# Narrow dilated attention: the values product as high and low parts at full width, with one raw buffer

## The chip, the cores and the metric

The kernel runs on one core of a Trainium2 chip. The metric is the device time of one execution in microseconds; three runs of the kernel before took 2870.96, 2873.74 and 2878.09 us, median 2873.74 us.

## The reference, cut to what matters

The program is two transformer blocks over 1024 tokens of width 1024, in float32. The second block has two attentions: a latent attention (8 heads) and a mixture of three dilated window attentions. The change touches two of the three dilated groups. Group g has 8 heads of 64 dimensions and dilation r = 1, 4 or 16; a query sees keys at offsets m*r with |m| <= 64:

```python
for g, (window, dilation) in enumerate(((128, 1), (512, 4), (2048, 16))):
    o, lse = dilated_group(q[:, :, sl], k[:, :, sl], v[:, :, sl], dilation, window // (2 * dilation))
# in dilated_group, per block of queries and its neighbourhood of keys:
s = where(valid, q @ k.T * D ** -0.5, NEG_INF)
m = max(s); p = exp(s - m); den = sum(p)
o = (p @ v) / den;  lse = m + log(den)
```

The groups' outputs are then mixed with a softmax over their lse.

## The kernel before, in words

Most of the kernel's work is projections. To keep float32 accuracy with float32r matmuls, both operands are split into a high part (a copy rounded to float32r, on ScalarE, L153) and a low part (the difference, on VectorE, L154), and three matmuls high x high, high x low, low x high are summed (L187 to L189). `kk.split` does the splitting.

The projections also serve as fill: `kk.fill` queues generators of projection matmuls, and `kk.pump(amount)` issues from them until the amount is used up (one step of three 512-column matmuls counts 3.0). The attention stages are traced in program order with a pump between their steps. The order of instructions on each engine is fixed before the run by a planner, which goes by priority (program order, with some blocks raised or lowered) and by when it expects an instruction's inputs and buffers to be ready; at run time each engine then works its queue strictly in that order and waits on semaphores.

The narrow dilated groups are computed by `dil_attention` (L1253), first for g = 1 (dilation 4, per = 12), then for g = 0 (dilation 1, per = 11). The widest group has a function of its own and isn't touched. Heads are taken in pairs, m = 0 to 3; the two heads of a pair lie on partitions 0 to 63 and 64 to 127. A unit (m, u) is two blocks of 128 queries of one pair; there are 16 units per group. For one unit:

- `scores` (L1314): 12 matmuls (64 rows each, the two heads side by side in the array) give for each of 4 (block, head) cells 256 key columns in PSUM; VectorE adds the mask and takes the maximum (L1334), ScalarE the exponential with its sum (L1336), into `d_p`.
- `turn` (L1340), once per head: four 128x128 transposes by TensorE (L146) into the one PSUM bank `pT`, then one copy into `d_pT`: on ScalarE for the first head (L1348), on VectorE for the second (L1346).
- `values` (L1353): 8 float32 matmuls into the bank `pO` (L1360), 128 keys by 64 value dimensions by 128 queries. Head 0 writes partitions 0 to 63, head 1 partitions 64 to 127. In the profile each stands as two records. In group 0 two neighbouring query blocks share the middle one of three key blocks; in group 1 both use the same two key blocks. ScalarE copies the result out (L1365, or L1370 with a stride for g = 1), and it is stored.

The loop (L1382) issues for each unit: transposes of head 0, a piece of preparation (queries at u = 0 and 2, keys of the next pair at u = 1, the load of the pair after next at u = 3), the next unit's scores, a pump, transposes of head 1, the values product of the unit before, and a pump. `load(m)` (L1269) loads keys, queries and values of a pair into double buffers (`dk_raw`, `dq_raw`, `dv`); two pairs are loaded before the loop. In group 0 GpSimd writes zeros into the two half blocks of values at the ends. `prep_k` (L1290) and `prep_q` (L1303) split keys and queries.

The forgetting attention of the first block and the latent attention of the second already compute their values product on split operands, with the value's high and low parts side by side in 128 weight columns (L550 to L552, L568) and the two halves of the result added on the way out (`pv_evac`, L521).

Of the kernel before, what the change touches and what calls it, by code (L numbers as in the profile page):

```python
# [1252 lines left out]
def dil_attention(kk, pool, C, g, qT, kT, v_d, od, nm_d, l_d, per):  # L1253
# [15 lines left out]
    def load(m):  # L1269
        rows = slice(m * P, m * P + P)  # L1270
        out = []
        for nm, src in (("dk_raw", kT), ("dq_raw", qT)):
            t = kk.t(pool, [P, S], F32, nm, 2)
            nc.sync.dma_start(t, src[rows, :])
            out.append(t)
        raws[m] = out
        v = kk.t(pool, [P, 9 - g, P], F32, "dv", 2)
        if g == 0:
            nc.gpsimd.memset(v[0:64, 0, :], 0.0)
            nc.gpsimd.memset(v[64:128, 8, :], 0.0)  # L1280
            nc.sync.dma_start(v[64:128, 0, :], v_d[0:64, rows])
            nc.sync.dma_start(v[:, 1:8, :], v_d[64 : 64 + 7 * P, rows].rearrange("(s p) c -> p s c", p=P))
            nc.sync.dma_start(v[0:64, 8, :], v_d[960:1024, rows])
        else:
            src = v_d[:, rows].rearrange("(h p r) c -> r p h c", r=4, p=P)
            for j in range(4):
                nc.sync.dma_start(v[:, 2 * j : 2 * j + 2, :], src[j])
        vals[m] = v

    def prep_k(m):  # L1290
        kh = kk.t(pool, [P, S + 2 * pad], F32R, "dKH", 2)
# [48 lines left out]
    def turn(pr, hh):  # L1340
        pt = kk.pT()
        for j in range(4):
            kk.transpose(pt[:, j * P : j * P + P], pr[:, hh * 512 + j * P : hh * 512 + j * P + P])
        pT = kk.t(pool, [P, 512], F32, "d_pT", 4 - g)
        if hh:
            nc.vector.tensor_copy(pT, pt)  # L1346
        else:
            nc.scalar.copy(pT, pt)  # L1348
        return pT

    outs = {}

    def values(m, u, pTs):  # L1353
        v = vals[m]
        po = kk.pO()
        for j in range(2):
            for w in range(2):
                blk = 2 * u + j + w if g == 0 else 2 * u + w
                for hh in range(2):
                    nc.tensor.matmul(po[half[hh], j * P : j * P + P], v[:, blk, half[hh]],  # L1360
                                     pTs[hh][:, (2 * j + w) * P : (2 * j + w + 1) * P], start=w == 0, stop=w == 1)
        rows = od[m * P : m * P + P, :]
        if g == 0:
            on = kk.t(pool, [P, 256], F32, "d_on", 2)
            nc.scalar.copy(on, po[:, :256])  # L1365
            nc.sync.dma_start(rows[:, u * 256 : u * 256 + 256], on)
            return
        if u == 0:
            outs[m] = kk.t(pool, [P, S], F32, "d_on", 1)
        nc.scalar.copy(perm(outs[m])[:, u, :], po[:, :256])  # L1370
        if u == 3:
            nc.sync.dma_start(rows, outs.pop(m))

    units = [(m, u) for m in range(4) for u in range(4)]
    load(0)
    prep_k(0)
    prep_q(0, 0)
    pr = scores(0, 0)
    load(1)
    kk.pump(40)  # L1380
    held = deque()
    for n, (m, u) in enumerate(units):  # L1382
        cur = pr
        nxt = units[n + 1] if n + 1 < len(units) else None
        pTs = []
        for hh in range(2):
            pTs.append(turn(cur, hh))
            if hh == 0:
                if u == 0:
                    prep_q(m, 1)  # L1390
                elif u == 1 and m < 3:
                    prep_k(m + 1)
                elif u == 2 and m < 3:
                    prep_q(m + 1, 0)
                elif u == 3 and m < 2:
                    load(m + 2)
                if nxt is not None:
                    pr = scores(*nxt)
            elif held:
                values(*held.popleft())  # L1400
            kk.pump(per)
        held.append((m, u, pTs))
    while held:
        values(*held.popleft())
# [380 lines left out]
```

## Time and profile before

| | |
|---|---|
| median of three runs | 2873.74 us |
| the profiled execution | 2867.28 us, span 2865.5 us |
| mean granted clock of TensorE | 0.996 of full |
| TensorE busy | 98% of the span, 14595 matmuls |
| VectorE, ScalarE, GpSimd busy | 44%, 37%, 8% |
| group 1 (g = 1) | about 1941 to 2092 us |
| group 0 (g = 0) | about 2126 to 2270 us |
| float32 values product L1360 | 512 records, 35.0 us busy, 279 ns mean |

How to read it: a record's duration holds the matmul's way through the pipeline, and records overlap; what a matmul costs is the distance from its start to the next one's start. Busy time of an engine is the union of its records. `pO<-d_pT,dv` is out<-in by the program's tile names. Weight loads (PEld) run beside the matmuls.

### The profile page before, as it was taken

Reading aid. Unit: us, or ns where it says so; the run is one execution under the profiler, and the core shown is the slowest. Engines: PE = TensorE matmul, PEld = TensorE weight load, DVE = VectorE, ACT = ScalarE, POOL = GpSimd, SP = SyncE. Lnnn points to the kernel's source line nnn. Section 1 sums busy time; section 2 is a strip of 40 time slices with the busy share of each in tenths; the row PEclk is TensorE's granted clock in tenths of the full one; section 3 lists DMA queues with packets and bytes.
Section 4 is the critical chain, followed back from the end, with each engine's and each line's share of the span. In section 5 each row is a group of like instructions: output and inputs, shape, how many; then the busy total and the mean of one; then the engine's idle time right before and its main releaser. Section 6 shows DMA issues by size and latency. Waiting matters only on the chain.

```text
span 2865.5 us, 37017 instructions
## 1 busy us (share of the span) xinstructions
PE 2814.2 (98%) x14595; PEld 2290.2 (80%) x14595; DVE 1253.8 (44%) x2072; ACT 1069.3 (37%) x1876; POOL 239.7 (8%) x321
## 2 busy tenths in 40 slices
PE   8999999999999999999999899999999999999998
PEld 6887788888888888888888778877777777888787
DVE  7144455545343222222315443535523366555553
ACT  4133555544131111111113331315547655555522
POOL 0012200000000000000000000000000165401100
PEclk9999999999999999999999999999999999999999
DMA  5112643255311111111113264543353355422641
GB/s 169 54 61 75 172 114 110 78 172 195 112 37 45 59 48 55 45 44 45 52 37 108 76 198 121 164 125 112 88 163 98 119 163 157 140 80 76 194 150 59
DMA packets 216327, 298.65 MB, mean 104 GB/s; under 512 B 34180, under 2 KB 137284, under 8 KB 216152
## 3 DMA queue, kind: packets, MB, share of 16 engines
q1 hardware_dynamic: 206104, 267.15, 30.2%
q0 software_dynamic: 10048, 29.13, 3.4%
q8 instruction: 114, 1.87, 0.3%
q14 instruction: 61, 0.50, 0.1%
HBM read 212.73 MB, written 81.36 MB: 103 GB/s over the span
## 4 chain that ended last, share of the span: by engine, by line
PE 93%; DMA 2%; DVE 2%; issue 1%; ACT 1%; POOL 0%; SPq 0%; POOLq 0%; ACTq 0%; DVEq 0%
PE pA L187 10%; PE pA L189 10%; PE pA L188 9%; PE pS L187 9%; PE pS L189 9%; PE pS L188 9%; PE pX L187 8%; PE pX L189 8%; PE pX L188 8%; PE pT L146 4%; PE pO L568 3%; PE pO L1360 1%; PE pS L1325 1%; PE pS L709 1%; PE pS L710 1%
## 5 line engine op out<-in xcount | busy, mean ns | idle before, releaser
L154 DVE TENSOR_TENSOR wl<-wraw,wh 128x1024 fp32r<-128x1024 f32 (+3 forms) x208 | 250.6, 1207 | 282.2 <-ACT wh L153 281.3
L153 ACT CAST wh<-wraw 128x1024 fp32r<-128x1024 f32 (+3 forms) x208 | 213.6, 1031 | 399.5 <-PE pA L189 238.3
L187 PE MATMUL pS<-big,wh 128*128 128x512 f32 x704 | 277.8, 395 | 0.0
L189 PE MATMUL pS<-big,wl 128*128 128x512 f32 x704 | 277.0, 393 | 0.0
L188 PE MATMUL pS<-big,wh 128*128 128x512 f32 x704 | 275.9, 392 | 0.0
L187 PE MATMUL pA<-big,wh 128*128 128x512 f32 x656 | 266.0, 405 | 0.2 <-ACT fm_out L733 0.2
L189 PE MATMUL pA<-big,wl 128*128 128x512 f32 x656 | 259.2, 395 | 0.0
L188 PE MATMUL pA<-big,wh 128*128 128x512 f32 x656 | 258.2, 394 | 0.0
L267 POOL TENSOR_TENSOR rs_r<-rs_v,mhalf 128x1 f32<-128x1 f32 (+3 forms) x64 | 61.3, 959 | 1523.8 <-DVE rs_v L266 1125.6
L154 DVE TENSOR_TENSOR ptl<-pT,pth 128x512 fp32r<-128x512 f32 (+2 forms) x184 | 116.1, 631 | 162.5 <-ACT pth L153 162.1
L187 PE MATMUL pX<-big,wh 128*128 128x512 f32 x432 | 175.0, 405 | 4.7 <-DVE dp L1012 3.5
L187 PE MATMUL pX<-wh,big 128*128 128x512 f32 (+2 forms) x448 | 171.5, 383 | 1.4 <-ACT l_x L1050 1.4
L187 PE MATMUL pA<-wh,big 128*128 128x512 f32 (+2 forms) x448 | 170.6, 381 | 0.0
L189 PE MATMUL pX<-big,wl 128*128 128x512 f32 x432 | 170.2, 394 | 0.0
L189 PE MATMUL pX<-wh,big 128*128 128x512 f32 (+2 forms) x448 | 169.3, 378 | 0.6 <-DVE big L154 0.6
L188 PE MATMUL pX<-big,wh 128*128 128x512 f32 x432 | 169.7, 393 | 0.0
L189 PE MATMUL pA<-wh,big 128*128 128x512 f32 (+2 forms) x448 | 169.3, 378 | 0.0
L188 PE MATMUL pX<-wl,big 128*128 128x512 f32 (+2 forms) x448 | 169.0, 377 | 0.1
L188 PE MATMUL pA<-wl,big 128*128 128x512 f32 (+2 forms) x448 | 168.3, 376 | 0.0
L189 PEld LDWEIGHTS pS<-big,wl 128*128 128x128 f32 x704 | 132.2, 188 | 31.3
L188 PEld LDWEIGHTS pS<-big,wh 128*128 128x128 f32 x704 | 132.5, 188 | 30.4
L187 PEld LDWEIGHTS pS<-big,wh 128*128 128x128 f32 x704 | 132.2, 188 | 29.4 <-ACT big L153 0.2
(426 smaller groups left out, 5736.4 us busy)
## 6 DMA issues: line engine op xcount, KB each, us to landing
wraw<-in_w_in_dram SPq DMA_DIRECT2D x96, 512.0 KB
wraw<-in_w_gate_dram SPq DMA_DIRECT2D x22, 512.0 KB
wraw<-in_w_up_dram SPq DMA_DIRECT2D x22, 512.0 KB
wraw<-in_w_down_dram SPq DMA_DIRECT2D x22, 512.0 KB
wraw<-in_w_out_dram SPq DMA_DIRECT2D x16, 512.0 KB
gT<-fm_out SPq DMA_DIRECT2D x32, 256.0 KB
ld<-gT SPq DMA_DIRECT2D x32, 256.0 KB
dq<-dp SPq DMA_DIRECT2D x96, 64.0 KB
```

What stands on the lines that cost most here:

```text
L146: self.nc.tensor.transpose(out, src, self.ident)
L153: self.nc.scalar.copy(h, src)
L154: self.nc.vector.tensor_tensor(l, src, h.bitcast(F32), op=ALU.subtract)
L187: mm(out, lhs[0], rhs[0], start=start, stop=False)
L188: mm(out, lhs[0], rhs[1], start=False, stop=False)
L189: mm(out, lhs[1], rhs[0], start=False, stop=stop)
L267: nc.gpsimd.tensor_tensor(r[:, :n], v[:, :n], self.mhalf[:, :n], op=ALU.pow)
L568: nc.tensor.matmul(po[:, c0:256], v2[:, kb + j, :], pr[m][:, j, c0:], start=kb == 0 and j == 0 and m == 0, stop=last and j == 1 and m == 1)
L709: nc.tensor.matmul(ps[:, c0:c1], q2[:, qs], k2[:, c0:c1], start=True, stop=False)
L710: nc.tensor.matmul(ps[:, c0:c1], qb[:, qs], kb_[:, c0:c1], start=False, stop=not last)
L1325: nc.tensor.matmul(ps[:, o : o + 256], q[half[hh], q0 : q0 + P], k[half[hh], k0 : k0 + 256], start=i == 0, stop=i == 2)
L1360: nc.tensor.matmul(po[half[hh], j * P : j * P + P], v[:, blk, half[hh]], pTs[hh][:, (2 * j + w) * P : (2 * j + w + 1) * P], start=w == 0, ...
```

## The change

- The values of a pair are split once into `dvhl`: for each head and key block 64 high and 64 low columns, float32r, 128 weight columns in all (`prep_v`, at u = 0 of the pair, after the last values product of the pair before).
- `turn` splits the transposed block into `d_ph` and `d_pl` (copy on ScalarE, subtraction on VectorE), for both heads.
- `values` runs float32r matmuls with 128 weight columns, one per (head, key block, high or low p). In group 0 the shared middle key block serves both query blocks in one 256-column matmul and the outer two have 128 columns: 12 matmuls per unit. In group 1 all 8 have 256 columns. The high half of the result lies on partitions 0 to 63 and the low half on 64 to 127; per head ScalarE copies the low half out (`d_lo`) and VectorE adds the two into the output tile.
- Keys, then values of a pair use one raw buffer `dk_raw` in turn, and `dq_raw` is single too. The values' load comes after the key split (`load_vals` at u = 1 for the next pair), the next pair's keys and queries are loaded after the values' split (`load(m + 1)` at u = 0). Nothing of a second pair is loaded before the loop.
- In the loop the values product comes ahead of the second head's transposes, with the pump in front of it.

```diff
--- before.py
+++ after.py
@@ -1270,11 +1270,14 @@
         rows = slice(m * P, m * P + P)
         out = []
         for nm, src in (("dk_raw", kT), ("dq_raw", qT)):
-            t = kk.t(pool, [P, S], F32, nm, 2)
+            t = kk.t(pool, [P, (9 - g) * P], F32, nm, 1)[:, :S]
             nc.sync.dma_start(t, src[rows, :])
             out.append(t)
         raws[m] = out
-        v = kk.t(pool, [P, 9 - g, P], F32, "dv", 2)
+
+    def load_vals(m):
+        rows = slice(m * P, m * P + P)
+        v = kk.t(pool, [P, (9 - g) * P], F32, "dk_raw", 1).rearrange("p (b c) -> p b c", c=P)
         if g == 0:
             nc.gpsimd.memset(v[0:64, 0, :], 0.0)
             nc.gpsimd.memset(v[64:128, 8, :], 0.0)
@@ -1286,6 +1289,13 @@
             for j in range(4):
                 nc.sync.dma_start(v[:, 2 * j : 2 * j + 2, :], src[j])
         vals[m] = v
+
+    def prep_v(m):
+
+        v2 = kk.t(pool, [P, 9 - g, 2, P], F32R, "dvhl", 1)
+        src = vals[m].rearrange("p b (h d) -> p b h d", h=2)
+        kk.split(v2[:, :, :, 0:64], v2[:, :, :, 64:128], src)
+        vals[m] = v2
 
     def prep_k(m):
         kh = kk.t(pool, [P, S + 2 * pad], F32R, "dKH", 2)
@@ -1341,64 +1351,81 @@
         pt = kk.pT()
         for j in range(4):
             kk.transpose(pt[:, j * P : j * P + P], pr[:, hh * 512 + j * P : hh * 512 + j * P + P])
-        pT = kk.t(pool, [P, 512], F32, "d_pT", 4 - g)
-        if hh:
-            nc.vector.tensor_copy(pT, pt)
-        else:
-            nc.scalar.copy(pT, pt)
-        return pT
+        ph = kk.t(pool, [P, 4, P], F32R, "d_ph", 3)
+        pl = kk.t(pool, [P, 4, P], F32R, "d_pl", 3)
+        kk.split(ph, pl, pt.rearrange("p (j q) -> p j q", j=4))
+        return ph, pl
 
     outs = {}
 
     def values(m, u, pTs):
+
         v = vals[m]
         po = kk.pO()
-        for j in range(2):
-            for w in range(2):
-                blk = 2 * u + j + w if g == 0 else 2 * u + w
-                for hh in range(2):
-                    nc.tensor.matmul(po[half[hh], j * P : j * P + P], v[:, blk, half[hh]],
-                                     pTs[hh][:, (2 * j + w) * P : (2 * j + w + 1) * P], start=w == 0, stop=w == 1)
+        for hh in range(2):
+            o = po[:, hh * 256 : hh * 256 + 256]
+            both = o.rearrange("p (j q) -> p j q", j=2)
+            if g == 0:
+                steps = [(2 * u, o[:, 0:P], lambda x: x[:, 0, :]), (2 * u + 1, both, lambda x: x[:, 1:3, :]),
+                         (2 * u + 2, o[:, P:256], lambda x: x[:, 3, :])]
+                steps = [steps[1], steps[0], steps[2]]
+            else:
+                steps = [(2 * u + w, both, lambda x, w=w: x.rearrange("p (j w) q -> p j w q", w=2)[:, :, w, :]) for w in range(2)]
+            for n, (blk, dst, at) in enumerate(steps):
+                for i in range(2):
+                    nc.tensor.matmul(dst, v[:, blk, hh, :], at(pTs[hh][i]), start=n == 0 and i == 0,
+                                     stop=n == len(steps) - 1 and i == 1)
+        los = []
+        for hh in range(2):
+            lo = kk.t(pool, [64, 256], F32, f"d_lo{hh}" if g == 0 else "d_lo", 1)
+            nc.scalar.copy(lo, po[64:128, hh * 256 : hh * 256 + 256])
+            if g == 0:
+                los.append(lo)
+                continue
+            if u == 0 and hh == 0:
+                outs[m] = kk.t(pool, [P, S], F32, "d_on", 1)
+            nc.vector.tensor_tensor(perm(outs[m])[half[hh], u, :], po[0:64, hh * 256 : hh * 256 + 256], lo, op=ALU.add)
         rows = od[m * P : m * P + P, :]
         if g == 0:
             on = kk.t(pool, [P, 256], F32, "d_on", 2)
-            nc.scalar.copy(on, po[:, :256])
+            for hh in range(2):
+                c = slice(hh * 256, hh * 256 + 256)
+                nc.vector.tensor_tensor(on[half[hh], :], po[0:64, c], los[hh], op=ALU.add)
             nc.sync.dma_start(rows[:, u * 256 : u * 256 + 256], on)
             return
-        if u == 0:
-            outs[m] = kk.t(pool, [P, S], F32, "d_on", 1)
-        nc.scalar.copy(perm(outs[m])[:, u, :], po[:, :256])
         if u == 3:
             nc.sync.dma_start(rows, outs.pop(m))
 
     units = [(m, u) for m in range(4) for u in range(4)]
     load(0)
     prep_k(0)
+    load_vals(0)
     prep_q(0, 0)
     pr = scores(0, 0)
-    load(1)
     kk.pump(40)
     held = deque()
     for n, (m, u) in enumerate(units):
         cur = pr
         nxt = units[n + 1] if n + 1 < len(units) else None
-        pTs = []
-        for hh in range(2):
-            pTs.append(turn(cur, hh))
-            if hh == 0:
-                if u == 0:
-                    prep_q(m, 1)
-                elif u == 1 and m < 3:
-                    prep_k(m + 1)
-                elif u == 2 and m < 3:
-                    prep_q(m + 1, 0)
-                elif u == 3 and m < 2:
-                    load(m + 2)
-                if nxt is not None:
-                    pr = scores(*nxt)
-            elif held:
-                values(*held.popleft())
-            kk.pump(per)
+        pTs = [turn(cur, 0)]
+        if u == 0:
+            prep_q(m, 1)
+        elif u == 1 and m < 3:
+            prep_k(m + 1)
+            load_vals(m + 1)
+        elif u == 2 and m < 3:
+            prep_q(m + 1, 0)
+        if nxt is not None:
+            pr = scores(*nxt)
+        kk.pump(per)
+        if held:
+            values(*held.popleft())
+        if u == 0:
+            prep_v(m)
+            if m < 3:
+                load(m + 1)
+        pTs.append(turn(cur, 1))
+        kk.pump(per)
         held.append((m, u, pTs))
     while held:
         values(*held.popleft())
```

## Rows read from the trace of the kernel before

**Rows 1.** The page's busy times: us (share of the span) and instructions, by engine.
```profile
PE 2814.2 (98%) x14595; PEld 2290.2 (80%) x14595; DVE 1253.8 (44%) x2072; ACT 1069.3 (37%) x1876; POOL 239.7 (8%) x321
```

**Rows 2.** Windows: stretch in us, busy us by engine, granted clock, DMA.
```profile
1950.00:2092.00 142.00, 142.00 (x963) 112.75 (x963) 81.32 (x198) 68.76 (x171) 1.57 (x12) 1.00 0.33 93
2140.00:2270.00 130.00, 129.96 (x900) 102.67 (x899) 46.32 (x144) 103.70 (x211) 2.24 (x13) 1.00 0.28 87
```

**Rows 3.** TensorE's waits from 1880 to 2320 us: us in total, times, longest.
```profile
PE pS L187 <- ACT QH L153: 2.2, 1, 2.2
PE pS L189 <- DVE QL L154: 0.4, 1, 0.4
```

**Rows 4.** TensorE's timeline in a unit of group 0: start us, us, line, count.
```profile
2173.16 0.60 PE L146 MATMUL pT<-ident,d_p 128*128 128x128 f32 x4
2173.68 1.09 PE L1360 MATMUL pO<-d_pT,dv 128*64 128x128 f32 x16
2174.71 0.50 PE L187 MATMUL pA<-big,wh 128*128 128x512 f32 x1
```

**Rows 5.** TensorE's timeline in the latent attention: transposes, float32r products.
```profile
2420.12 0.60 PE L146 MATMUL pT<-ident,prob 128*128 128x128 f32 x4
2420.48 0.48 PE L187 MATMUL pS<-KH,QH 96*128 96x512 f32 x1
...
2421.95 0.28 PE L568 MATMUL pO<-pth,v_hl 128*128 128x256 f32 x1
...
2422.42 0.40 PE L187 MATMUL pX<-big,wh 128*128 128x512 f32 x1
```

**Rows 6.** TensorE's timeline on the forgetting attention's diagonal: 128-column products.
```profile
355.52 0.22 PE L568 MATMUL pO<-pth,v_hl 128*128 128x128 f32 x1
355.58 0.27 PE L568 MATMUL pO<-ptl,v_hl 128*128 128x128 f32 x1
355.69 0.45 PE L187 MATMUL pA<-big,wh 128*128 128x512 f32 x1
```

**Rows 7.** ScalarE by line, group 0: count | busy us, mean ns | idle before.
```profile
L731 ACT ACT_TABLE_LOAD x15 | 19.2, 1283 | 0.3
...
L1348 ACT COPY d_pT<-pT 128x512 f32<-128x512 f32 x15 | 8.8, 585 | 11.4 <-PE pT L146 11.3
...
L1365 ACT COPY d_on<-pO 128x256 f32<-128x256 f32 x16 | 5.7, 359 | 5.0 <-issue 3.4 <-ACT d_p L1336 1.2 <-ACT fm_out L731 0.5
L731 ACT ACTIVATE fm_out<-pA 128x512 f32<-128x512 f32 x8 | 4.8, 598 | 0.1
```

**Rows 8.** ScalarE and VectorE by line, whole run: splits, low halves, additions.
```profile
L154 DVE TENSOR_TENSOR wl<-wraw,wh 128x1024 fp32r<-128x1024 f32 x194 | 238.1, 1229 | 244.5 <-ACT wh L153 244.0
L153 ACT CAST wh<-wraw 128x1024 fp32r<-128x1024 f32 x194 | 202.9, 1048 | 375.4 <-PE pA L189 218.5 <-PE pA L188 78.2 <-PE pS L188 64.5
...
L154 DVE TENSOR_TENSOR ptl<-pT,pth 128x512 fp32r<-128x512 f32 x152 | 104.7, 689 | 145.6 <-ACT pth L153 145.2
...
L527 DVE TENSOR_TENSOR pv_o<-pO,pv_lo 64x256 f32<-64x256 f32 x64 | 26.1, 408 | 4.4 <-ACT pv_lo L526 4.3
...
L526 ACT COPY pv_lo<-pO 64x256 f32<-64x256 f32 x64 | 23.6, 369 | 22.5 <-PE pO L568 21.5
```

**Rows 9.** Loads: queue and ScalarE timelines for keys; chain of waits, next stage.
```profile
1880.27 1.07 SPq L1274 DMA_DIRECT2D dk_raw<-dk  x2
...
1885.01 3.98 ACT L153 CAST dKH<-dk_raw 128x1024 fp32r<-128x1024 f32 x2 [11.65 <-DMA dk_raw<-dk]
...
2279.48 6.49 DMA raw<-knT
```

**Rows 10.** Chain that ended last, in group 1: start us, us, engine, line.
```profile
1972.00 0.44 PE pT L146 x4
...
1976.42 0.44 PE pT L146 x4
```

**Rows 11.** VectorE by line, group 1: one of the projections' rotation steps.
```profile
L1018 DVE TENSOR_TENSOR dp<-pA,cos 128x512 f32<-128x512 f32 x8 | 5.6, 696 | 0.1
```

## The prediction

> **What bounds the kernel now.** I read the page first: TensorE is busy 98% of the span, VectorE 44%, ScalarE 37% [rows 1]. Then the two stretches that the change touches, group 1 (1950 to 2092 us) and group 0 (2140 to 2270 us). The reader should see that TensorE is busy for all of both at the full granted clock, so that a microsecond of TensorE work taken out there shortens the run, and that the evacuating engines are not equally free: ScalarE is busy 69 of 142 us in group 1 but 104 of 130 us in group 0, VectorE 81 of 142 and 46 of 130 [rows 2]. Then TensorE's waits from 1880 to 2320 us: two rows, 2.6 us, and both belong to the attention that follows [rows 3]. So the dilated groups hide their whole chain (mask, exponential, transposes, copies) behind the projections' matmuls mixed in. What counts is (a) TensorE time per unit, a unit being two query blocks of one head pair, 16 per group, and (b) whether the longer chain still hides.
>
> **TensorE, per unit.** A unit now runs its second four transposes, then the values product, then projections. From start to start: transposes at 2173.16, product at 2173.68, projection at 2174.71, so 0.52 + 1.03 = 1.55 us [rows 4]. After the change the product is entered from projections and the transposes follow it. Four transposes ahead of a 128-wide float32r matmul take only 0.36 us (2420.12 to 2420.48) [rows 5]; ahead of the 64-wide float32 product they cost 0.16 us more. What comes behind is a projection in both orders, so its start-up stays out of the sum.
>
> In group 1 the new product has 8 matmuls of 256 columns. The same form runs four in 0.47 us (2421.95 to 2422.42) [rows 5], so 0.94 us. With the transposes 1.30 us, 0.25 less than now: 16 x 0.25 = 4.0 us gained.
>
> In group 0 each head has two matmuls of 256 columns and four of 128. The only 128-column float32r matmuls with 128-wide weights in this trace are on the forgetting attention's masked diagonal: the first is followed after 0.06 us, the second after 0.11 [rows 6]. I read this as sets of weights that can't be loaded closer than some 0.11 us apart: one 128-column matmul can borrow from the longer ones before it, the next can't. Per head that is 2 x 0.12 + 0.06 + 3 x 0.11 = 0.63 us, for two heads 1.26. With the transposes 1.62 us, 0.07 more than now: 16 x 0.07 = 1.1 us lost. The bound on the good side is every 128-column matmul at 0.06 us: 4 x 0.12 + 8 x 0.06 = 0.96 us, 1.32 with the transposes, 16 x 0.23 = 3.7 us gained; on the bad side each at 0.11: 0.1 us more per unit, 2.7 us lost. I take the 1.1 us loss, since four such matmuls in a row are nearest to the 0.11 us row. Net: 4.0 - 1.1 = 2.9 us gained, at best 7.7, at worst 1.3. The half-width float32 was not as dear as its form suggests: the whole product for both heads took 1.03 us.
>
> The Trainium skill ("TensorE: Matmul & The Clock Gate", Back-to-back issue gap) gives about 81 ns per matmul of 128 columns in a stream with weight loads. By it group 0's product would take about 8 x 0.081 + 4 x 0.12 = 1.13 us and the group would gain 1.0 us instead of losing 1.1: an estimate from that page, 5.0 us in all. The rows speak for the slower figure.
>
> **ScalarE and VectorE.** Added per unit: the second block's copy moves to ScalarE (0.59 us) and each block gets a subtraction of 0.69 us on VectorE, where one copy of the same 512 columns goes; two copies of low halves (0.37 us each) replace one output copy (0.36 in group 0), and two additions of 0.41 us are new on VectorE [rows 7, 8]. In group 1 the additions write with a stride; I allow them up to the 0.69 us of a step twice as wide. Per head pair one split of values is new, 1152 columns in group 0 and 1024 in group 1: by the 1024-column rows about 1.05 to 1.2 us on ScalarE and 1.23 to 1.4 us on VectorE [rows 8].
> - Group 0: ScalarE 16 x 0.59 + 32 x 0.37 - 16 x 0.36 + 4 x 1.16 = 20 us more, 124 of 130 us (95%); VectorE 16 x 0.69 + 32 x 0.41 + 4 x 1.35 = 30 us more, 76 of 130.
> - Group 1: ScalarE at most 20 us more, 89 of 142; VectorE 11.0 + 13 to 22 + 5 = 29 to 38 us more, 110 to 119 of 142 (80%).
>
> None of it is TensorE's, and I cost it at nothing: the projections' matmuls between the halves of a unit cover it. Part of ScalarE's idle time in group 0 is mere earliness (11.4 us ahead of the transposed copies [rows 7]) and can be filled. If that cover goes, the price is in the first rival.
>
> **Loads.** The same DMAs are issued (keys and queries one each per head pair, values three or four, and in group 0 two fills of zeros by GpSimd), but the next pairs' loads no longer run a whole head pair ahead. With one raw buffer, keys and queries are issued when the values' split has freed it, the values when the keys' split has. Both become waits on the DMA queue; behind them stand output stores, projection stores and weight loads, which have two, three and three buffers. The key split waits on ScalarE for its load, and behind it may stand the next unit's exponentials. Keys (512 KB) were issued at 1880.27 and split from 1885.01, 4.7 us; a load of 256 KB in the next stage shows as 6.5 us [rows 9]. I cost this at nothing, with the second rival as bound. The values' own load has three units to land.
>
> **The sum.** The profiled run took 2867.28 us (span 2865.5); the median of three runs is 2873.74, 6.5 us above, which is the spread between executions. 2867.3 - 2.9 = 2864.4 us for an execution like it; on the median 2873.7 - 2.9 = 2870.8 us.
>
> **Rivals.**
> 1. *Transposes wait for their one bank (slower).* Now a block is copied out in one step, and the product stands between a unit's second transposes and the next unit's first: they start at 1972.00 and 1976.42, 4.4 us apart [rows 10]. Afterwards the product is gone from there: 4.4 - 1.0 - 0.2 = 3.2 us, and in it must fit transposes of about 0.6 us to their end, copy 0.59, subtraction 0.69 and two hand-overs (0.1 us each, my estimate): 2.1 us. Slack 1.1 us. In group 0 a table load and a gating evacuation (1.28 + 0.60 us) stand once per unit on ScalarE [rows 7]; ahead of that copy they overrun by 0.8 us, 16 x 0.8 = 13 us. In group 1 every second projection evacuation brings four VectorE steps of 0.69 us [rows 11]: 2.76 - 1.1 = 1.7 us over, 8 times, 13 us. If half of them fall in the other, roomier half of the unit, 13 us in all: 2870.8 + 13 = 2884 us; if all hit, 2897. For it: ScalarE at 95%. Against it: no such wait now at 80%, and the order is planned ahead, so projections can be put in front of late transposes. It decides from 1.1 us of delay on. The Trainium skill ("Trainium Kernel Development and Optimization", Best Practices) warns that tiling TensorE better does not speed up PSUM evacuation; that would be this rival.
> 2. *The key load is late.* The values' split (2.5 us) ends 0.7 us before the next unit begins (3.2 us after the product), the load lands 4.7 to 6.5 us later, then split (1.05 us, up to twice that with a stride) and exponentials (2 us, in group 0 a table load too) end 8 to 10 us into a unit of some 8.7 us (15 copies in 130 us [rows 7]): up to 1.5 us late, three times per group, at most 9 us: 2880 us. Against it: with the exponentials queued ahead of the split, nothing is late.
> 3. *Weights don't limit the 128-column matmuls.* 7.7 us gained: 2866.0 us.
>
> **Chances.** Forecast (2863 to 2879 us, by the product's bounds and some lateness) 0.56; first rival, alone or with the second, 0.23; second alone 0.10; third 0.11. About 0.3% (8.6 us) either way is what a measurement of this kernel can tell from no change: below 2865.1 or above 2882.4 us. Faster: a third of the third rival and the forecast's lower edge, 0.13. Slower: the first and the worst of the second, 0.26. The same: 0.61. For the range I go down to 2861 (third rival, less some of the runs' spread) and up to 2891 (between half and all of the first rival's delays).
>
> **What would show it.** In the profile after: group 1's product of 8 records in about 0.94 us, group 0's of 12 in about 1.26 us (0.96 would be the third rival); 0.36 us for the transposes behind it; no rows of TensorE waiting for the subtraction of the low half (rival 1) or, at a head pair's second unit, for exponentials behind a key split (rival 2); ScalarE near 95% busy in group 0. The forecast is wrong if TensorE's waits inside the two groups exceed some 8 us, or if its sum per unit differs from 1.30 and 1.62 us by more than 0.2 us.

## The result, and the profile after

The changed kernel takes 2903.99 us (median of 4 runs, 2899.42 to 2908.97) against 2872.84 for the kernel before (4 runs): ratio 1.0109, 95% interval [1.0095, 1.0123]. It is slower by 1.1%, outside the range that the prediction gave. The profiled execution took 2908.97 us (span 2907.2), that of before 2867.28 (span 2865.5); the spans lie 41.7 us apart, the medians 31.2. In the later sessions the kernel before took 2871.9 to 2872.8 us, so the experiments' times can be set beside these.

The page's busy times, beside [rows 1]:

```profile
PE 2829.6 (97%) x14403; PEld 2305.1 (79%) x14403; DVE 1321.6 (45%) x2176; ACT 1102.4 (38%) x1946; POOL 237.1 (8%) x321
```

TensorE has 192 instructions fewer than before, as the change intends, and is busy 15 us longer, so the count does not explain the loss. The two dilated groups show where the span went. The windows below run from each group's first transposes to its last product (columns as in [rows 2]), first in the kernel before, then in the changed one:

```profile
1951.20:2090.00 138.80, 138.80 (x948) 110.52 (x947) 81.32 (x198) 67.79 (x168) 0.41 (x2) 1.00 0.32 92
2136.30:2268.80 132.50, 132.46 (x917) 104.90 (x917) 48.17 (x152) 105.96 (x212) 2.24 (x13) 1.00 0.29 93
```

```profile
1952.20:2103.70 151.50, 141.16 (x821) 115.08 (x820) 114.72 (x249) 85.43 (x204) 0.83 (x8) 0.98 0.34 99
2149.90:2298.80 148.90, 139.40 (x855) 113.30 (x853) 77.00 (x203) 122.66 (x246) 2.09 (x14) 1.00 0.31 97
```

Group 1 grew by 12.7 us and group 0 by 16.4, together 29.1 of the 41.7 us. Before, TensorE was busy in all of both; now it is idle for 10.3 us in group 1 and 9.5 in group 0, and in group 1 the granted clock is no longer 1.00. The other engines got about the work that was forecast (ScalarE 17.6 and 16.7 us more, forecast up to 20 and 20; VectorE 33.4 and 28.8, forecast 29 to 38 and 30), and neither is full: VectorE 76% in group 1, ScalarE 82% in group 0.

TensorE's waits from 1880 to 2340 us, beside [rows 3], name what it waits for:

```profile
PE pT L146 <- DVE d_pl L154: 19.7, 18, 3.0
PE pS L187 <- ACT QH L153: 5.7, 1, 5.7
```

The first row is new: 18 times the next transposes wait for the subtraction that reads the one bank last, 7 times in group 1 (10.3 us) and 11 times in group 0 (9.4 us). All 18 stand between a unit's second transposes and the next unit's first. That is the first rival, with its mechanism as written: the bank is given back too late.

Why it is late shows on the two engines. In group 1 the longest wait follows the second transposes that start at 1956.51. On ScalarE, behind the exponentials, which end at 1957.35:

```profile
1957.97 2.04 ACT L153 CAST dKH<-dk_raw 128x1024 fp32r<-128x1024 f32 x1 [0.62 <-DMA dk_raw<-dk]
1959.88 0.61 ACT L153 CAST d_ph<-pT 128x512 fp32r<-128x512 f32 x1
```

and on VectorE:

```profile
1960.04 1.98 DVE L154 TENSOR_TENSOR dKL<-dk_raw,dKH 128x1024 fp32r<-128x1024 f32 x1 [1.44 <-ACT dKH L153]
1961.95 0.67 DVE L1018 TENSOR_TENSOR dp<-pA,cos 128x512 f32<-128x512 f32 x1
1962.55 0.67 DVE L154 TENSOR_TENSOR d_pl<-pT,d_ph 128x512 fp32r<-128x512 f32 x1
```

The next pair's key split (2.04 us, and it waits for its load too) stands on ScalarE ahead of the copy of the transposed block; its low half (1.98 us) stands on VectorE ahead of the subtraction. The transposes had ended by 1957.1; the subtraction ends at 1963.2. On TensorE that becomes a hole, with the next transposes put among the next unit's scores:

```profile
1960.01 0.28 PE L1335 MATMUL pS<-dKL,dQH 64*128 64x256 f32 x1
1963.27 0.66 PE L146 MATMUL pT<-ident,d_p 128*128 128x128 f32 x4 [2.98 <-DVE d_pl L154]
```

This is one wait of the seven, 3.0 of 10.3 us. The next two in length (2.41 and 2.47 us) have no key split. ScalarE's copy starts 2.9 us after the transposes' end, behind exponentials, a weight split and a low-half copy, and then the subtraction waits on VectorE. Ahead of the one that ends the wait of 2.47 us, with the transposes over at 2054.95, stand the low half of the query split, rotation steps of the projections, and both additions of the product before:

```profile
2056.51 1.08 DVE L1321 SCALAR_TENSOR_TENSOR dQL<-dq_raw,dQH 128x512 fp32r<-128x512 f32 x1
2057.50 0.70 DVE L1018 TENSOR_TENSOR dp<-pA,cos 128x512 f32<-128x512 f32 x1
2058.10 0.62 DVE L1387 TENSOR_TENSOR d_on<-pO,d_lo 64x256 f32<-64x256 f32 x1
2058.53 0.70 DVE L1019 TENSOR_TENSOR dp<-dp,dp 128x512 f32<-128x512 f32 x1
2059.27 0.60 DVE L1387 TENSOR_TENSOR d_on<-pO,d_lo 64x256 f32<-64x256 f32 x1
2059.90 0.69 DVE L154 TENSOR_TENSOR d_pl<-pT,d_ph 128x512 fp32r<-128x512 f32 x1
```

Of the other four, 0.4 to 0.8 us long, three stand behind the low half of the values' split (1.2 us on VectorE) and one behind a weight split's. Rotation steps stand there in all seven, the two additions in six.

In group 0 no key split need be there. A unit's second transposes start at 2162.80, and ScalarE does this:

```profile
2161.88 1.28 ACT L731 ACT_TABLE_LOAD   x1
2163.17 0.60 ACT L731 ACTIVATE fm_out<-pX 128x512 f32<-128x512 f32 x1
2163.79 1.28 ACT L1346 ACT_TABLE_LOAD   x1
...
2166.20 0.64 ACT L1381 COPY d_lo<-pO 64x256 f32<-64x256 f32 x2
2166.87 0.59 ACT L153 CAST d_ph<-pT 128x512 fp32r<-128x512 f32 x1
```

A gating evacuation between two table loads, two exponentials and the two new copies of low halves come first; the copy starts 3.5 us after the transposes' end, and the next transposes (2168.50) wait 1.36 us. A gating evacuation or one of the two table loads around it comes between transposes and copy in 8 of the 11 waits of this group, the copies and additions of low halves in 10.

TensorE's own terms of the sum can be read from one product of each group. Group 1, changed kernel:

```profile
2026.79 0.28 PE L1376 MATMUL pO<-d_ph,dvhl 128*128 128x256 f32 x1
...
2027.74 0.60 PE L146 MATMUL pT<-ident,d_p 128*128 128x128 f32 x4
2028.10 0.48 PE L187 MATMUL pA<-big,wh 128*128 128x512 f32 x1
```

Group 0:

```profile
2161.49 0.28 PE L1376 MATMUL pO<-d_ph,dvhl 128*128 128x256 f32 x1
2161.61 0.28 PE L1376 MATMUL pO<-d_pl,dvhl 128*128 128x256 f32 x1
2161.73 0.23 PE L1376 MATMUL pO<-d_ph,dvhl 128*128 128x128 f32 x1
2161.79 0.27 PE L1376 MATMUL pO<-d_pl,dvhl 128*128 128x128 f32 x1
2161.90 0.27 PE L1376 MATMUL pO<-d_ph,dvhl 128*128 128x128 f32 x1
2162.01 0.28 PE L1376 MATMUL pO<-d_pl,dvhl 128*128 128x128 f32 x1
...
2162.80 0.62 PE L146 MATMUL pT<-ident,d_p 128*128 128x128 f32 x4
2163.18 0.47 PE L187 MATMUL pA<-big,wh 128*128 128x512 f32 x1
```

Product 0.95 and 1.31 us (forecast 0.94 and 1.26), transposes behind it 0.36 and 0.38: 1.31 and 1.69 us per unit against 1.55 before [rows 4]. Group 1 gains 16 x 0.24 = 3.8 us of TensorE work, group 0 loses 16 x 0.14 = 2.2.

### The profile page after: what moved, and what is told of

It is laid out like the page before. It is cut to its first block, busy times and chain, and to the rows that moved or that the text cites. A ratio compares the mean times of both kernels' runs of the same rounds, so it can differ in the third digit from the quotient of the medians.

```text
span 2907.2 us, 36838 instructions
## 1 busy us (share of the span) xinstructions
PE 2829.6 (97%) x14403; PEld 2305.1 (79%) x14403; DVE 1321.6 (45%) x2176; ACT 1102.4 (38%) x1946; POOL 237.1 (8%) x321
## 4 chain that ended last, share of the span: by engine, by line
PE 88%; DVE 4%; ACT 3%; DMA 2%; issue 2%; POOL 0%; SPq 0%; POOLq 0%; ACTq 0%; DVEq 0%
PE pA L187 9%; PE pA L189 9%; PE pA L188 9%; PE pS L187 9%; PE pS L189 9%; PE pS L188 9%; PE pX L187 7%; PE pX L189 7%; PE pX L188 7%; PE pT L146 4%; PE pO L568 3%; PE pS L709 1%; ACT d_p L1346 1%; PE pS L710 1%; PE pO L1376 1%
## 5 line engine op out<-in xcount | busy, mean ns | idle before, releaser
L931 DVE TENSOR_TENSOR silu<-silu,pS 128x512 f32<-128x512 f32 x44 | 30.2, 686 | 285.3 <-ACT silu L930 285.3
L188 PEld LDWEIGHTS pS<-big,wh 128*128 128x128 f32 x704 | 132.5, 188 | 30.4
```

The lines of the kernel that those rows point to most:

```text
L188: mm(out, lhs[0], rhs[1], start=False, stop=False)
L931: nc.vector.tensor_tensor(s, s, ps[:, 512:], op=ALU.mult)
```

## The experiments

Three theories, as the expectations letter them. A: the bank is late because of what stands ahead of the copy and the subtraction in the two engines' queues, and of where the transposes stand (A2: the queue order alone). B: the loads of the single raw buffer are late. C: the longer chain itself, or ScalarE's load, doesn't fit, whatever the order. Group times are from each profiled run, counted as in the windows above. Every edit makes the planner lay out the queues anew, so a run can differ from its neighbour in more than the lines shown.

**1. Raise the split of the transposed block.**

```
-        kk.split(ph, pl, pt.rearrange("p (j q) -> p j q", j=4))
+        with kk.tc.high_priority(offset=HP):
+            kk.split(ph, pl, pt.rearrange("p (j q) -> p j q", j=4))
```

> The changed kernel with one edit: in turn() the split of the transposed block (ScalarE copy, VectorE subtraction) is raised in the planner's priority, as the other attentions do it. Theory A (the transposes wait until the one transpose bank has been copied and subtracted, 19.7 us of waits on the low half in the changed kernel, and stalls bring stretches of half clock): those waits fall below 5 us, the groups lose some 25 of their 28 us, and the whole comes out within 6 us of the kernel before. Theory B (late loads of keys) and theory C (the new product and its evacuation cost TensorE or ScalarE time whatever the order): still 20 us or more above the kernel before.

Measured 2893.70 us (2889.03 to 2894.03), 1.0077 [1.0064, 1.0090] of before: 10 us better than the change, far from all of it. Group 1 144.5 us, group 0 145.7. Still 12 waits on the subtraction, 14.6 us, the longest 3.7. In group 1 the additions no longer stand ahead of the subtraction in any of the three waits left. One still stands behind the key split (3.7 us), the other two behind the query split's low half and rotation steps (1.1 us each); in group 0 a gating evacuation or one of its table loads comes before the copy in 8 of 9. As I read it, priority decides only between work that the planner sees ready at once. So A missed as it was put, and C stood open.

**2. Give the bank back after ScalarE's copy.** The low part of the probabilities is left out (it becomes zero), with the same instructions.

```
-        kk.split(ph, pl, pt.rearrange("p (j q) -> p j q", j=4))
+        nc.scalar.copy(ph, pt.rearrange("p (j q) -> p j q", j=4))
+        nc.vector.tensor_tensor(pl, ph.bitcast(F32), ph.bitcast(F32), op=ALU.subtract)
```

> The changed kernel with the low half made from the copied high half alone (high minus high, so the low part of the probabilities is left out); VectorE does as much work, but the bank is free after ScalarE's copy. Theory A in the form that VectorE's subtraction is what comes late: the waits vanish, the time falls by 20 us or more. Theory A in the form that ScalarE's copy already comes late (in group 0 it starts 1 to 4 us after the transposes): the waits move from the subtraction to the copy; group 1 gains most of its 12.6 us, group 0 keeps more than half of its 16 us; total some 12 to 18 us faster than the changed kernel. Theories B and C: unchanged within 5 us.

Measured 2884.55 us, 1.0050 [1.0036, 1.0065], 19 us better than the change, where B and C had no more than 5. Group 1 takes 137.1 us, 1.7 less than before the change; group 0 145.6. The waits are now on ScalarE's copy:

```profile
PE pT L146 <- ACT d_ph L1356: 9.1, 10, 1.5
```

So in group 1 it was mostly VectorE's subtraction that came late, in group 0 mostly ScalarE's copy (7 of these 10 waits, 7.3 us, are there).

**3. The loads alone.** The kernel before, with one raw buffer each for keys and queries and the loads where the change has them. The values keep buffers of their own, so the next keys' load doesn't wait for a values' split as it does in the change.

```
-            t = kk.t(pool, [P, S], F32, nm, 2)
+            t = kk.t(pool, [P, S], F32, nm, 1)
...
-    load(1)
...
-                elif u == 3 and m < 2:
-                    load(m + 2)
...
+                if u == 0 and m < 3:
+                    load(m + 1)
```

> The kernel before with the loads alone changed: single raw buffers for keys and queries, the next pair's keys and queries loaded at its first unit and the values after the key split, the product still float32 with its own values buffer. Theory A: within 3 us of the kernel before. Theory B (late loads): 8 us or more slower, with TensorE waiting behind key splits.

Measured 2870.25 us, 0.9999 [0.9988, 1.0009]. Both groups are as before to 0.1 us:

```profile
1950.50:2089.30 138.80, 138.80 (x948) 110.55 (x947) 81.37 (x198) 68.28 (x168) 1.56 (x12) 1.00 0.35 100
2135.60:2268.20 132.60, 132.55 (x919) 105.00 (x917) 48.15 (x152) 106.00 (x212) 1.62 (x12) 1.00 0.32 99
```

Later loads into single buffers cost nothing here, and B and the second rival are out for that part. The buffer shared by keys and values is not in this run. In the changed kernel it has a share in the longest wait: there the key split stood idle on ScalarE for 0.62 us until its load came.

**4. Group 1 new with the raised split, group 0 old.** `dil_attention(kk, pool, C, 0, ...)` calls the old function.

> Group 1 (dilation 4) in the changed form with the split raised as in e1_split_first, group 0 in the form of the kernel before. Theory A: group 1's product and transposes cost 0.25 us less per unit and nothing is late, so 2 to 5 us faster than the kernel before (ratio 0.998 to 0.999). Theory C: not faster, 3 us or more slower.

Measured 2876.99 us, 1.0019 [1.0010, 1.0029]. Group 0 is back at 132.5 us; group 1 takes 143.9, not under 138.8: three waits are left (5.2 us, the longest 3.0), and the longest is the one behind the key split. The effects are separate by group, but A's number failed again; 4.8 us slower than before is C's.

**5. More distance after the second transposes.**

```
-        kk.pump(per)
+        kk.pump(per - 4)
...
         pTs.append(turn(cur, 1))
-        kk.pump(per)
+        kk.pump(per + 4)
```

> The changed kernel with the projection work between the two transposes of a unit moved: some four 512-column matmuls (about 0.95 us) fewer between the first head's transposes and the second head's, as many more between the second head's and the next unit's first. Theory A (the short distance after the second head's transposes, 3.2 us, is what the bank's release overruns): the waits on the subtraction d_pl fall from 19.7 us to under 9, both groups shorten, and the time is 2884 to 2893 us, 10 to 20 us under the changed kernel's 2904. Theory C (ScalarE as a whole has no time left, so the copy is late wherever the transposes stand): group 0 stays within 3 us of its 148.9 us, the waits only move to the other distance, and the time is within 6 us of 2904.

Measured 2898.21 us (2892.30 to 2901.06), 1.0083 [1.0066, 1.0100]. Group 0 shortened by 6.9 us to 142.0 (waits 9.4 to 4.7 us), group 1 by 2.1 only, to 149.4. Neither theory's numbers: A's fell short, and group 0 moved more than C allows. Distance matters in group 0; in group 1, where waits of 2.9, 1.9 and 1.9 us are left, what is late is late by more than another microsecond.

**6. No low halves in group 0.** The two copies and the additions are left out there; VectorE copies the high halves.

```
-            lo = kk.t(pool, [64, 256], F32, f"d_lo{hh}" if g == 0 else "d_lo", 1)
+            if g == 0:
+                continue
+            lo = kk.t(pool, [64, 256], F32, "d_lo", 1)
             nc.scalar.copy(lo, po[64:128, hh * 256 : hh * 256 + 256])
...
-                nc.vector.tensor_tensor(on[half[hh], :], po[0:64, c], los[hh], op=ALU.add)
+                nc.vector.tensor_copy(on[half[hh], :], po[0:64, c])
```

> The changed kernel without the low halves in group 0: ScalarE's two copies of the low half and the additions are left out there, VectorE copies the high half out in place of each addition (so the products' low parts don't reach the output); TensorE's instructions are the same. Theory C (ScalarE's load of two more copies per unit makes its copy of the transposed tile late in group 0): group 0 shortens from 148.9 to under 141 us, and the time is 8 us or more under 2904. Theory A (order and distance of the transposes, not the load): group 0 stays within 4 us of 148.9, time 2899 to 2905. Group 1 stays as it was (151.5) under both.

Measured 2897.04 us, 1.0087 [1.0069, 1.0104]: 7 us under the change. Group 0 141.1 us (7.8 less), its waits 9.4 to 3.1 us; group 1 unchanged at 151.8. That is C's side, just short of its numbers: the low halves' way out counts in group 0, but half of the loss stays. The run takes away ScalarE's copies and VectorE's wait for them together, so it doesn't say which of the two counts.

**7. Distance in group 1 alone.** Experiment 4 with the shift of experiment 5, the next key split put in the program behind the second transposes.

```
-        elif u == 1 and m < 3:
-            prep_k(m + 1)
-            load_vals(m + 1)
...
         pTs.append(turn(cur, 1))
+        if u == 1 and m < 3:
+            prep_k(m + 1)
+            load_vals(m + 1)
```

> New layout in group 1 alone (group 0 as in the kernel before), with the high and low copies raised in priority, the projection work shifted by four matmuls as in the run beside it, and the next key split put behind the second head's transposes, not ahead of the scores. Theory A: no wait on d_pl above 1 us is left in group 1, so no stretch at half clock either; group 1 takes 137 to 139 us against 138.8 before, and the time is 2866 to 2872, at or up to 0.2% under the kernel before. Theory C (any place of the transposes finds an engine late): waits of 1 to 3 us stay, group 1 takes 141 to 145 us and the time is 2874 to 2879 as in the run without the shift (2877.0).

Measured 2876.86 us, 1.0010 [1.0001, 1.0019], group 1 145.1 us: C's numbers. But the trace does not show C. Behind the second transposes at 1955.72, ScalarE again does

```profile
1958.48 2.01 ACT L153 CAST dKH<-dk_raw 128x1024 fp32r<-128x1024 f32 x1 [0.79 <-DMA dk_raw<-dk]
1960.39 0.57 ACT L153 CAST d_ph<-pT 128x512 fp32r<-128x512 f32 x1
```

and TensorE waits 3.5 us. The planner had moved the split ahead of the copy in spite of its place in the program, presumably since it expected it to be ready sooner. At run time it was not: the transposes ended at 1956.32, and ScalarE still stood idle for 0.79 us until the split's load came. The order itself had not been tried yet.

**8. The order, by force.** The next pair's queries move to u = 1, its keys to u = 2; both large splits are queued on each engine behind the last copy and subtraction written so far.

```
+    def behind(ctx, k):
+        ins = kk.nc.cur_bb.bb.instructions
+        for e in (mybir.EngineType.Activation, mybir.EngineType.DVE):
+            ctx.enter_context(kk.tc.issue_after(next(i for i in reversed(ins) if i.engine == e)))
...
         pTs.append(turn(cur, 1))
+        with ExitStack() as ctx:
+            behind(ctx, n)
+            if u == 0:
+                prep_v(m)
...
+            if u == 2 and m < 3:
+                prep_k(m + 1)
```

> New layout in group 1 alone (group 0 as in the kernel before), raised copies and shifted projection work as in the run before it, and now the two large splits of a pair (keys: 2.0 us on each engine; values: 1.2 us) queued on ScalarE and VectorE behind the second head's copy and subtraction, by an order of issue. Theory A2 (it is the engines' queue order: one large split ahead of the copy makes the bank late): no wait on d_pl above 1 us, no half clock inside the group, group 1 takes 135 to 138 us against 138.8 before (own matmuls 3.4 us less), and the time is 2865 to 2871. Theory C (the chain of copy and subtraction itself doesn't fit): waits of 2 us and more stay and the time is 2873 to 2878.

Measured 2871.27 us (11 runs), 0.9996 [0.9987, 1.0005]. Group 1, then the unchanged group 0:

```profile
1951.70:2089.60 137.90, 135.97 (x821) 112.50 (x820) 113.09 (x249) 85.72 (x204) 1.63 (x12) 1.00 0.37 109
2135.80:2268.40 132.60, 132.56 (x919) 105.00 (x917) 48.18 (x152) 106.03 (x212) 2.24 (x13) 1.00 0.29 93
```

No wait for the bank is left in group 1, ScalarE and VectorE are as busy as in the change (85.7 and 113.1 us against 85.4 and 114.7), and the group is 13.6 us shorter than there. The copy now stands first and the key split after it:

```profile
2008.87 0.59 ACT L153 CAST d_ph<-pT 128x512 fp32r<-128x512 f32 x1
2009.35 2.06 ACT L153 CAST dKH<-dk_raw 128x1024 fp32r<-128x1024 f32 x1
```

The time is 0.3 us above A2's band, the group inside it. For group 1 that shuts out C: the same work and the same chain fit without a wait for the bank once the order is right. Two things changed together, though, the forced order and the key split's move to u = 2, by when its load has landed; no run separates them. What is left there is three short waits for the key split's low half, now later:

```profile
PE pS L1490 <- DVE dKL L154: 1.9, 3, 0.7
```

**9. All three orders in both groups, without group 0's low halves** (experiments 6 and 8 together).

> New layout in both groups with all three orders (raised copies, shifted projection work, large splits behind the copies), and in group 0 without the low halves: ScalarE's copies of them and the additions are left out, VectorE copies the high halves. Both groups then show TensorE's own work: group 1 135 to 138 us, group 0 133.5 to 136 us (before 132.5; product and transposes 1 to 2.5 us dearer), time 2866 to 2873. If group 0 stays above 139 us, something other than order, distance and the low halves' copies makes its bank late.

Measured 2875.62 us, 1.0010 [1.0001, 1.0019], 2.6 us above the expected band. Group 1 137.9, group 0 136.7 us, just above its band too.

**10. The same with the low halves: the changed kernel whole, in the better order.**

> The changed kernel whole, with all three orders in both groups. Group 1 as in the run with group 1 alone, 135 to 138 us. Theory A2 (queue order alone): group 0 133.5 to 137 us as well, time 2867 to 2873. Theory C for group 0 (its ScalarE, with the low halves' copies, has too little time left): group 0 139 to 145 us, 4 us or more above the run without the low halves, time 2874 to 2884.

Measured 2882.06 us, 1.0033 [1.0021, 1.0045], 22 us better than the change. Its groups, and then group 0 of experiment 9:

```profile
1956.00:2093.90 137.90, 135.95 (x820) 112.47 (x819) 113.29 (x249) 85.73 (x204) 0.83 (x8) 1.00 0.38 109
2140.10:2279.50 139.40, 135.98 (x855) 112.64 (x852) 76.52 (x203) 122.40 (x246) 2.02 (x14) 1.00 0.33 104
```

```profile
2138.90:2275.60 136.70, 135.20 (x854) 112.89 (x852) 76.75 (x203) 111.57 (x216) 2.02 (x14) 1.00 0.34 106
```

Group 0's 139.4 us and the time are C's numbers, but the distance to experiment 9 is 2.7 us and not C's 4 or more. Of group 0's 16.4 us, order and distance give back 9.5 (148.9 to 139.4), and the low halves' 10.8 us on ScalarE, together with the additions, are worth 2.7 more. The 4.2 us that stay in experiment 9 against before are the 2.2 us of dearer product, 1.4 us of short waits (three rows: 0.6, 0.6 and 0.2), and some 0.6 that I can't place. In experiment 10 the group's waits are 3.4 us, 1.7 of them for the bank, 1.5 for key splits that now come later and 0.2 for exponentials.

**11 and 12. A version to beat both.** Experiment 8's group 1 was 0.9 us ahead of before, but its latent stage took 369.0 us against 361.5 (from the first score to the last product): the first exponential stood on ScalarE behind a key split waiting for its load, and TensorE waited 4.0 us. Both kernels got one more order there, the kernel before as control:

```
+    exps = next(i for i in reversed(kk.nc.cur_bb.bb.instructions) if i.engine == mybir.EngineType.Activation)
...
+                if not causal and h == 0:
+                    ctx.enter_context(kk.tc.issue_after(exps))
                 v[h + 1] = prep_k(h + 1)
```

> The kernel before with one order at the start of the latent attention: ScalarE's split of the second head's key is queued behind the first two exponentials (it waits for a load there, and stood ahead of them). In the kernel before the exponentials were ready only as the load came, so little is to be had: latent stage 359 to 362 us against 361.5, time within 3 us of the kernel before. If it gains 4 us or more, the load stood in the way there too.

> New layout in group 1 alone with the three orders of the run that tied the kernel before (2871.3), and the same order at the start of the latent attention as in the run beside it. Theory: that run's group 1 was 0.9 us shorter than before and lost it, with 7.5 us in the latent stage (369.0 against 361.5 us), to one wait of 4.0 us for the first exponential, which stood on ScalarE behind a key split that waited for its load, and to half clock behind it. With the order the latent stage takes 361 to 364 us and the time is 2863 to 2867, 0.998 of the kernel before. Rival: the stage's start waits for the loads themselves, whatever stands first on ScalarE; the latent stage stays at 366 us or more, time 2869 to 2873.

Measured: before with it 2872.06 us, 1.0001 [0.9992, 1.0010], as expected; experiment 8 with it 2872.13 us, 0.9994 [0.9985, 1.0003]. The wait of 4.0 us is gone from the second, but its latent stage is 365.2 us, between the theory's band and the rival's, and its time is the rival's: nothing is gained that can be told from no change. The best version is level with the kernel before.

## Why the prediction was wrong

- **Failed step:** "None of it is TensorE's, and I cost it at nothing: the projections' matmuls between the halves of a unit cover it." I had judged the cover by sums of busy time (95% and 80%). In sum it was there for group 1: experiment 8 runs it with the same engine work and no wait for the bank. It was not there at the place where it counts, since other work, up to 2.0 us in one piece and several pieces at a time, stood between the transposes and the bank's release: 18 waits, 19.7 us.
- **The first rival was what happened; I gave it 0.23.** Its slack was overrun 18 times in 32 units, each time in the distance that it named. It named gating evacuations with their table loads in group 0, which stand there in 8 of 11 waits, and rotation steps in every second unit of group 1, which stand there in all 7. Its price was 13 us for half, 26 us for all, and the waits came to 19.7 us; but even its dearest time, 2897, lies under the 2904 measured, since a wait cost more than its length (below) and the span grew outside the groups too. Its hand-overs, put at 0.1 us each, are 0.03 to 0.06 us in the trace. What it missed is what stood beside the work that it named. That is the change's own low-half copies and additions, in 16 of the 18 waits, and the splits of values, keys, queries and weights, 1.1 to 2.0 us each on VectorE. The key split made the longest single wait; the prediction used it for the loads' rival only, as something that waits, not as something that others wait behind. That "the order is planned ahead, so projections can be put in front of late transposes" was the argument against, and it failed: 15 of the 18 late transposes stood right behind a score of the next unit, and the planner put other work ahead of the copies, in experiment 7 even against the program's order. The sentence of the Trainium skill cited there ("Trainium Kernel Development and Optimization", Best Practices: better tiling of TensorE does not speed up PSUM evacuation) agrees with group 1, where product and transposes got 3.8 us cheaper and the bank's release cost 10.3. No run kept the product behind the second transposes as in the kernel before, so whether its low halves would then stay out of the bank's way is not known.
- **TensorE's terms** were right for group 1 (1.31 us per unit, forecast 1.30) and a little low for group 0 (1.69, forecast 1.62: 2.2 us lost, not 1.1). The 128-column matmuls stand 0.11 us apart behind the first, as the diagonal's row said. Four of them in a row take 0.39 us, 0.10 each. The third rival, at 0.06, is out. The Trainium skill's 81 ns ("TensorE: Matmul & The Clock Gate", Back-to-back issue gap) is not met in this stream.
- **Loads** at nothing: right for later loads into single buffers (experiment 3). In the changed kernel a late key load is 0.62 us of the longest wait, within the first rival and not as the second had it.
- **The sum.** Group 1: -3.8 us of work, +10.3 of waits, and about +3.3 of half clock (two stretches of 3.4 us at 0.50 and 0.52) make 9.8 of 12.7 us. Group 0: +2.2 of work and +9.4 of waits make 11.6 of 16.4. The other 7.7 us lie mostly in the scores: from each matmul's start to the next one's, less the waits, the 180 score records of a group take 16.4 us against 13.6 before in group 1 and 17.2 against 14.1 in group 0. The last matmul ahead of each wait, mostly a score, takes some 0.16 us more than one that has the next right behind it: 3 us for 18 waits. By the same working experiment 10 leaves only 2.2 us over (group 1: -0.9 + 3.8 - 2.0; group 0: 6.9 - 2.2 - 3.4 of waits), so most of them went with the waits.
- **Open.** The span has 12.6 us more outside the groups: 4.3 between group 0 and the latent attention's first score (a wait of 5.7 us in place of 2.2), 6.2 in that stage, which starts at half clock, and the rest elsewhere. That stage took 361.5 to 363.2 us in the three profiles with both groups old and 362.6 to 369.0 in those with a new group, with different waits for loads each time; experiment 12 took one away without gain. Why it tends to start later with the new groups is not settled.

## What to carry to other kernels

Where one bank is handed round, the bound is the distance between two uses of it against the chain that frees it, with all that may be queued ahead of each link, the longest single instruction first; the engines' busy share says little (VectorE at 82% in group 1 and no wait for the bank once the order was right, 76% and 10 us of waits when it wasn't). A step that the planner expects to be ready sooner can slip in ahead of such a link, whatever its place in the program: look in the trace where it was put, and pin it behind the link. The same goes for work that the change itself adds, here the low halves' copies and additions. Before adding chain length to two stages, price each by itself: here one of them could be had at no loss, the other not.

## What the runs showed of the hardware

A wait of TensorE costs more than its length where the clock falls behind it. Granted clock in the changed kernel behind the wait of 2.98 us that ends at 1963.27, in the stretch around the end of the wait of 5.7 us, at 2328.93, and, last, in the stretch right after the first (columns as in [rows 2]; the last but two is the granted clock):

```profile
1964.10:1967.50 3.40, 3.40 (x15) 2.69 (x14) 2.06 (x9) 2.24 (x8) 0.00 (x0) 0.50 0.32 83
...
2325.90:2332.70 6.80, 3.77 (x9) 2.99 (x10) 3.93 (x4) 1.05 (x1) 4.26 (x5) 0.50 1.03 303
1968.00:1971.40 3.40, 3.40 (x23) 3.01 (x22) 2.01 (x4) 1.08 (x3) 0.00 (x0) 1.00 0.56 157
```

At 0.50 (1.2 of 2.4 GHz) 512-column matmuls start 0.43 us apart, behind it 0.23:

```profile
1966.03 0.63 PE L189 MATMUL pX<-big,wl 128*128 128x512 f32 x1
1966.46 0.63 PE L187 MATMUL pX<-big,wh 128*128 128x512 f32 x1
...
1967.65 0.39 PE L187 MATMUL pX<-big,wh 128*128 128x512 f32 x1
1967.88 0.40 PE L188 MATMUL pX<-big,wh 128*128 128x512 f32 x1
```

The length of the wait alone does not decide. In group 1 of the changed kernel the clock fell behind the wait of 2.41 us that ends at 2021.27 (0.52 from 2022.30 to 2025.70) and not behind the one of 2.47 us that ends at 2060.74 (1.00 from 2060.80 to 2067.60). At the start of the latent attention both the kernel before and experiment 12 waited 2.2 us; the first stayed at 1.00, the second fell:

```profile
2294.00:2300.80 6.80, 5.73 (x23) 4.17 (x23) 5.51 (x5) 2.78 (x5) 6.11 (x8) 1.00 1.03 312
```

```profile
2293.00:2299.80 6.80, 6.30 (x15) 4.42 (x15) 4.15 (x4) 0.48 (x1) 5.06 (x8) 0.50 0.93 257
```
